# Order of the pairs in the two down projections and the mixer's output projection, and side sums added into the accumulating banks

## The chip, the cores and the metric

The kernel runs on one core of a Trainium2 chip. The metric is the device time of one execution in microseconds, as the median of several runs; lower is better. One more execution was profiled, and all rows below are from that one.

## The reference

One encoder layer on an input of 256 tokens by 2048 channels, in float32:

```
x = x + 0.5 * rms_norm((silu(a) * b) @ w_ffn1_down) * gain    # a, b = halves of rms_norm(x) @ w_ffn1_gate_up
h = rms_norm(x);  p = h @ w_mix_in                            # split into a recurrence and a window attention
x = x + rms_norm(concat(y_h, y_a) @ w_mix_out) * gain
x = x + 0.5 * rms_norm((silu(a) * b) @ w_ffn2_down) * gain    # the same again with second weights
```

The inner width of the feed-forward parts is 5632, so each down projection is a 256 x 5632 by 5632 x 2048 product; the output projection is 256 x 2048 by 2048 x 2048. Every product here is made of three: each operand is split into a high part (rounded to fp32r) and the low rest, and high x high, high x low and low x high are added.

## The kernel before

Weights stream from memory in tiles `raw` of 128 x 2048 (1 MB) through three buffers (`rawp`, L67). `split_half` makes of each half of such a tile a high part `h` on ScalarE (the cast, L168) and a low part `l` on VectorE (the subtraction, L169), in four buffers each (`hip`, `lop`, L68, L69). TensorE's results lie in the eight banks of PSUM, two tags (`pa`, `pb`) of four (L70).

The class `Pairs` (L413) runs the three projections above. The inner dimension is cut into units of 256 rows (a "pair" of 128-row blocks): 22 units in a down projection, 8 in the output projection. The 2048 output columns are done in two runs of 1024 (`begin(0)`, `begin(1)`), each over all units. One run has eight banks: four that become the result, `c[m][n]` (128 tokens by 512 columns each), and four side banks `p`.

- A **plain** unit (L462) is 8 block products into `c`, each of three matmuls: 24 matmuls of 512 columns.
- A **mixed** unit (`seven`, L468) does the same with 7 block products of sums of blocks (Strassen's scheme, Winograd's form): 21 matmuls. VectorE first makes four sums of weight blocks (`t` and a block of `raw` itself, L477 to L481); `h`, `l`, `th`, `tl` are split from those, and `sp` from sums of the left operand made earlier (`sums_of`). The tiles `t`, `th`, `tl` lie in the pool `far`, in the room of the previous stage's left operand `xt`. Four of the seven products go to the side banks `p`, three to `c`.
- The side banks reach the result through four sums `y` (`side_sums`, L511, after the first plain unit that follows the last mixed one) and four more additions `c + y` at the end of the run (`close`, L538), which also start the sum of squares for the norm on ScalarE (`jk`, L546).

In the down projections units 0, 2, ..., 16 are mixed and the order is 0 to 21, so a mixed unit comes first. In the output projection units 4 and 5 are mixed and the order is 4, 0, 5, 1, 6, 7, 2, 3.

`finish` (L574) does the second run: the last two units (`HELD`) are loaded ahead and done bank after bank (`products`), and after each bank come `close`, the product with the gain `pg` (`gains`, L602, all 2048 columns of `pg` loaded by one DMA at L586), the norm's factor `r` (`tot` L174, `v` L176 on VectorE, a power on GpSimd L178) and the update of the residual `X` (`update` L614 on VectorE, or `update_aside`, ScalarE L620 and GpSimd L621). Then `X` is turned on TensorE (L202) into the next stage's operand `xt` (high part L219 on ScalarE, low part L224 on VectorE), or stored (L632).

Outside `finish` the order on the engines is not written by hand: a scheduler at compile time orders each engine's instructions by program order and by its own model of when inputs and buffers are ready. Within the `manual_schedule` blocks of `finish` TensorE, VectorE and ScalarE keep the order of the text.

Of the kernel before, what the change touches and what calls it, by code (L numbers as in the profile page):

```python
# [36 lines left out]
def hymba_layer_kernel(  # L37
# [375 lines left out]
    class Pairs:  # L413
# [7 lines left out]
        def __init__(self, w, orders, tiles, sums, room):  # L421

            self.w, self.orders, self.tiles, self.sums = w, orders, tiles, sums
            self.room, self.post = room, None
# [7 lines left out]
        def begin(self, run):  # L432
            self.now, self.pos = run, 0
            order = self.orders[run]
            self.todo = [u for u in order if u in self.sums]
# [3 lines left out]
            some = len(self.todo)  # L439
# [6 lines left out]

        def bank(self, at):
            return self.p[at[1]] if at[0] == "p" else self.c[at[1]][at[2]]

        def three(self, at, ah, al, h, l):  # L450
            for lhs, rhs in ((ah, h), (ah, l), (al, h)):
                n = self.seen.get(at, 0)
                self.seen[at] = n + 1
                nc.tensor.matmul(  # L454
                    self.bank(at), lhs, rhs, start=(n == 0), stop=(n == self.of[at] - 1)
                )
# [54 lines left out]
        def side_sums(self):  # L511
# [16 lines left out]
            if not any(u in self.sums for u in self.orders[self.now]):  # L528
                return
            (y11, y12), (y21, y22) = y  # L530
            p1, p5, p6, p7 = self.p
            nc.scalar.copy(y11, p1)
            nc.vector.tensor_tensor(y12, p6, y11, ALU.add)
            nc.vector.tensor_tensor(y21, p7, y12, ALU.add)
            nc.vector.tensor_tensor(y12, p5, y12, ALU.subtract)
            nc.vector.tensor_tensor(y22, p5, y21, ALU.subtract)

        def close(self, m, n):  # L538
            q = 2 * self.now + n
            y = self.y[m, q]  # L540
            if any(u in self.sums for u in self.orders[self.now]):
                nc.vector.tensor_tensor(y, self.c[m][n], y, ALU.add)
            else:
                nc.vector.tensor_copy(y, self.c[m][n])
            jk = stat.tile([P, 512], BF16, tag="jk", name=nm("jk"), bufs=1)
            nc.scalar.activation(jk, y, AF.Square, accum_out=self.ssq[m][:, q : q + 1])  # L546

        def work(self, upto):

            order = self.orders[self.now]  # L550
            while self.pos < upto:
                u = order[self.pos]
                if u in self.sums:
                    self.seven(u)
                    self.todo.remove(u)
                else:
                    hs, ls = split_load(*self.source(u))
                    for k in range(2):
                        for m in range(2):
                            for n in range(2):  # L560
                                self.plain(u, hs, ls, m, n, k)
                    ready = not self.todo and (self.now == 0 or self.post)
# [794 lines left out]
```

## Time and profile before

| | us |
|---|---|
| median of 3 runs (1912.8 to 1914.1) | 1912.92 |
| the profiled execution | 1910.94 |
| its span, first to last instruction | 1909.2 |
| TensorE busy with matmuls | 1875.7 (98%) |
| VectorE busy | 1374.0 (72%) |
| ScalarE busy | 1048.9 (55%) |

The mean granted TensorE clock was 0.993 of full speed. Matmuls overlap in the profile: one of 512 columns is shown as 0.39 us long, and starts a good 0.22 us after the one before it. So TensorE's share cannot be read as work done; what is lost is seen as idle time before an instruction, or as too few matmuls in a stretch.

### The profile page before, as it was taken

To read this page: it belongs to the slowest core of one execution; us is meant where nothing else is said; L and a number is where in the kernel's file an instruction comes from. 1 tells how busy PE (TensorE), PEld (TensorE's weight loads), DVE (VectorE), ACT (ScalarE), POOL (GpSimd) and SP (SyncE) were. 2 spreads that over 40 slices of the span, in tenths; PEclk is the share of its full clock that TensorE was granted. 3 is DMA by queue.
4 is the path that set the end of the run, shared out by engine and by line. 5 is a ranking of instruction groups with operands and counts; after the bars stand their busy time and mean duration, and the time that the engine had idled before them with its cause. 6 is when DMAs were issued, how large, how long until landed. Compare 5 with 4: busy or idle time off the path is not lost.

```text
span 1909.2 us, 25425 instructions
## 1 busy us (share of the span) xinstructions
PE 1875.7 (98%) x10080; PEld 1620.0 (85%) x10080; DVE 1374.0 (72%) x1785; ACT 1048.9 (55%) x1452; POOL 38.7 (2%) x49
## 2 busy tenths in 40 slices
PE   9999999999999999999999899999999999999997
PEld 7888888888788887888888688888888888888886
DVE  6765666666698987577778787666666656598996
ACT  6544444444465656578668656544444444465553
POOL 1000000000000002000000001000000000000001
PEclk9999999999999999999999899999999999999999
DMA  7655555555465574555455455555555655465663
GB/s 245 199 196 191 188 183 193 198 177 197 156 220 199 200 285 164 199 180 165 158 182 166 148 211 199 190 186 184 192 197 176 198 191 185 155 220 200 212 252 130
DMA packets 267736, 365.92 MB, mean 192 GB/s; under 512 B 6376, under 2 KB 233792, under 8 KB 266464
## 3 DMA queue, kind: packets, MB, share of 16 engines
q1 hardware_dynamic: 267264, 364.15, 56.9%
q8 instruction: 79, 1.29, 0.3%
q14 instruction: 41, 0.34, 0.1%
q0 software_dynamic: 352, 0.14, 0.0%
HBM read 360.06 MB, written 4.21 MB: 191 GB/s over the span
## 4 chain that ended last, share of the span: by engine, by line
PE 55%; issue 41%; DVE 2%; DMA 1%; ACT 0%; POOL 0%; SPq 0%; DVEq 0%; ACTq 0%; POOLq 0%
PE pa L285 16%; PE pb L285 9%; PE pa L290 8%; PE pa L454 6%; PE pb L454 5%; PE pb L290 5%; PE pa L380 1%; PE pa L378 1%; PE pa L379 1%; DVE X L614 0%; PE pb L1094 0%; PE pb L1072 0%; PE pb L202 0%; PE pa L328 0%; DMA X<-in_x_dram 0%
## 5 line engine op out<-in xcount | busy, mean ns | idle before, releaser
L169 DVE TENSOR_TENSOR l<-raw,h 128x1024 fp32r<-128x1024 f32 x664 | 797.5, 1221 | 392.0 <-issue 288.6
L168 ACT CAST h<-raw 128x1024 fp32r<-128x1024 f32 x664 | 694.1, 1055 | 478.0 <-PE pa L285 155.7
L285 PE MATMUL pa<-xt,h 128*128 128x512 f32 x2048 | 500.2, 392 | 0.0
L285 PEld LDWEIGHTS pa<-xt,h 128*128 128x128 f32 x2048 | 375.8, 188 | 72.2
L285 PE MATMUL pb<-xt,h 128*128 128x512 f32 x1392 | 340.5, 391 | 0.0
L285 PEld LDWEIGHTS pb<-xt,h 128*128 128x128 f32 x1392 | 255.3, 188 | 49.5 <-DVE R L254 0.5
L290 PEld LDWEIGHTS pa<-xt,l 128*128 128x128 f32 x2048 | 263.5, 191 | 9.9
L290 PE MATMUL pa<-xt,l 128*128 128x256 f32 x2048 | 270.2, 284 | 0.0
L454 PE MATMUL pa<-h,ht 128*128 128x512 f32 x560 | 201.4, 392 | 5.5 <-ACT h L168 5.5
L290 PEld LDWEIGHTS pb<-xt,l 128*128 128x128 f32 x1392 | 178.5, 191 | 6.8
L290 PE MATMUL pb<-xt,l 128*128 128x256 f32 x1392 | 180.6, 283 | 0.0
L454 PE MATMUL pb<-h,ht 128*128 128x512 f32 x416 | 144.6, 389 | 0.0
L454 PEld LDWEIGHTS pa<-h,ht 128*128 128x128 f32 x560 | 105.9, 189 | 28.3 <-ACT h L168 6.4
L454 PE MATMUL pa<-l,ht 128*128 128x512 f32 x280 | 110.0, 393 | 1.1 <-DVE l L169 1.1
L454 PEld LDWEIGHTS pb<-h,ht 128*128 128x128 f32 x416 | 78.1, 188 | 16.3
L726 ACT COPY u<-pb 128x256 f32<-128x256 f32 x88 | 28.5, 376 | 110.8 <-PE pb L285 110.8
L726 ACT COPY z<-pa 128x256 f32<-128x256 f32 x88 | 28.8, 376 | 96.7 <-PE pa L285 95.8
L454 PE MATMUL pb<-l,ht 128*128 128x512 f32 x208 | 80.9, 389 | 0.0
L169 DVE TENSOR_TENSOR tl<-t,th 128x1536 fp32r<-128x1536 f32 x40 | 70.2, 1754 | 5.1 <-ACT th L168 5.0
L454 PE MATMUL pa<-h,sp 128*128 128x512 f32 x160 | 64.4, 402 | 5.1 <-ACT sp L168 4.6
L168 ACT CAST th<-t 128x1536 fp32r<-128x1536 f32 x40 | 59.2, 1481 | 13.7 <-DVE t L481 13.4
L454 PEld LDWEIGHTS pa<-l,ht 128*128 128x128 f32 x280 | 52.9, 189 | 13.0 <-DVE l L169 2.2
(245 smaller groups left out, 1705.8 us busy)
## 6 DMA issues: line engine op xcount, KB each, us to landing
raw<-in_w_ffn_gate_up_dram SPq DMA_DIRECT2D x175, 1024.0 KB, 5.0
raw<-in_w_ffn_down_dram SPq DMA_DIRECT2D x88, 1024.0 KB, 4.9
raw<-in_w_mix_in_dram SPq DMA_DIRECT2D x52, 1024.0 KB, 5.0
raw<-in_w_mix_out_dram SPq DMA_DIRECT2D x16, 1024.0 KB, 5.0
X<-in_x_dram SPq DMA_DIRECT2D x2, 1024.0 KB, 8.6
pg<-in_post_norm_ffn_dram SPq DMA_DIRECT2D x2, 1024.0 KB, 10.5
bias<-row SPq DMA_DIRECT2D x16, 128.0 KB, 3.9
kept<-X SPq DMA_DIRECT2D x2, 1024.0 KB, 4.1
```

The source lines that it names most:

```text
L168: nc.scalar.copy(hi, src)
L169: nc.vector.tensor_tensor(lo, src, hi.bitcast(F32), ALU.subtract)
L285: nc.tensor.matmul(slot[f], weights(hs, kk, f), xcol(xt, k), start=(k == 0), stop=(k == KT - 1))
L290: nc.tensor.matmul(slot[f][:, 0:T], weights(ls, kk, f), xcol(xt, kh * 8 + kk, 0), start=False, stop=False,)
L378: nc.tensor.matmul(dst, xh, h[:, o : o + n], start=(k == 0), stop=False)
L379: nc.tensor.matmul(dst, xh, l[:, o : o + n], start=False, stop=False)
L380: nc.tensor.matmul(dst, xl, h[:, o : o + n], start=False, stop=(k == KT - 1))
L454: nc.tensor.matmul(self.bank(at), lhs, rhs, start=(n == 0), stop=(n == self.of[at] - 1))
L726: nc.scalar.copy(z[:, f, :], banks[f][:, T : 2 * T])
```

## The change

1. Orders. In a down projection a plain unit comes first, then mixed and plain units in turn: 1, 0, 3, 2, 5, 4, ..., 15, 14, 17, 16, then 18 to 21 (in the second run 15, 14, 17, 16 the same, so that units under 14 stay ahead of the others). In the output projection the first run is 0, 1, 4, 6, 5, 7, 2, 3 and the second 0, 4, 1, 5, 6, 7, 2, 3.
2. `fold` replaces `side_sums`: it makes the same four sums and adds each into its bank `c[m][n]` in place, on VectorE, between the first (`after`) and the second plain unit behind the last mixed one. In those two units the products are sorted by bank, so that six matmuls of one bank stand together.
3. `close` goes. `squares` reads the bank itself on ScalarE, `gains` multiplies the bank with the gain on VectorE. The first run's gains are done at its end, and not in `finish`. `pg` is loaded in two halves, the first at the start of the first run.
4. `finish`: the same replacement within the hand-written orders; at the very end all four updates of `X[:, 0]` go to VectorE, behind `squares(1, 0)`, the last row's banks are multiplied in place in PSUM, and ScalarE with GpSimd update `X` for (1, 0) in place of (1, 3).

The number of matmuls does not change, nor that of VectorE's additions of banks (four sums and four additions a run) and of gains.

```diff
         def begin(self, run):
...
-            self.todo = [u for u in order if u in self.sums]
+            self.after = max(i for i, u in enumerate(order) if u in self.sums) + 1
...
-        def side_sums(self):
+        def half_gain(self, pool):
+            pg = pool.tile([P, 1024], F32, tag="pg", name=nm("pg"), bufs=1)
+            cs = slice(self.now * 1024, (self.now + 1) * 1024)
+            nc.sync.dma_start(pg, self.gain_src[0:1, cs].broadcast_to([P, 1024]))
+            self.pg = pg
+
+        def fold(self):
...
+            add = nc.vector.tensor_tensor
+            c = self.c
             nc.scalar.copy(y11, p1)
-            nc.vector.tensor_tensor(y12, p6, y11, ALU.add)
-            nc.vector.tensor_tensor(y21, p7, y12, ALU.add)
-            nc.vector.tensor_tensor(y12, p5, y12, ALU.subtract)
-            nc.vector.tensor_tensor(y22, p5, y21, ALU.subtract)
-
-        def close(self, m, n):
+            add(y12, p6, y11, ALU.add)
+            add(c[0][0], c[0][0], y11, ALU.add)
+            add(y21, p7, y12, ALU.add)
+            add(y12, p5, y12, ALU.subtract)
+            add(c[0][1], c[0][1], y12, ALU.add)
+            add(c[1][0], c[1][0], y21, ALU.add)
+            add(y22, p5, y21, ALU.subtract)
+            add(c[1][1], c[1][1], y22, ALU.add)
+
+        def squares(self, m, n):
+            jk = stat.tile([P, 512], BF16, tag="jk", name=nm("jk"), bufs=1)
             q = 2 * self.now + n
-            y = self.y[m, q]
-            if any(u in self.sums for u in self.orders[self.now]):
-                nc.vector.tensor_tensor(y, self.c[m][n], y, ALU.add)
...
-            nc.scalar.activation(jk, y, AF.Square, accum_out=self.ssq[m][:, q : q + 1])
+            nc.scalar.activation(
+                jk, self.c[m][n], AF.Square, accum_out=self.ssq[m][:, q : q + 1]
+            )
+
+        def gains(self, m, n, dst=None):
+            if dst is None:
+                dst = self.y[m, 2 * self.now + n]
+            nc.vector.tensor_tensor(
+                dst, self.c[m][n], self.pg[:, n * 512 : (n + 1) * 512], ALU.mult
+            )
...
                     hs, ls = split_load(*self.source(u))
...
+                    if self.pos == self.after + 1:
+                        self.fold()
+                    places = [(k, m, n) for k in range(2) for m in range(2) for n in range(2)]
+                    if self.pos in (self.after, self.after + 1):
+
+                        places.sort(key=lambda at: at[1:])
+                    for k, m, n in places:
+                        self.plain(u, hs, ls, m, n, k)
                 self.pos += 1
 
         def first_run(self):
+            self.half_gain(self.room)
             self.work(len(self.orders[0]))
             for m in range(2):
                 for n in range(2):
-                    self.close(m, n)
+                    self.squares(m, n)
+                    self.gains(m, n)
             self.begin(1)
...
+                def in_place(n):
+                    gains(1, n, dst=self.c[1][n])
+                    y[1, 2 + n] = self.c[1][n]
+
                 with tc.manual_schedule(engines=ordered):
...
+                    products(0, 0, every)
+                    squares(0, 0)
+                    gains(0, 0)
+                    products(0, 1, every)
+                    squares(0, 1)
+                    gains(0, 1)
+                    products(1, 0, every)
+                    squares(1, 0)
+                    for q in range(4):
+                        update(0, q)
+                    in_place(0)
+                    products(1, 1, every)
+                    squares(1, 1)
+                    in_place(1)
                     for q in range(4):
                         store(0, q)
-                    update_aside(1, 3)
-                    for q in range(3):
+                    update_aside(1, 0)
+                    for q in (1, 2, 3):
                         update(1, q)
                         store(1, q)
-                    store(1, 3)
+                    store(1, 0)
...
-            rows = Pairs(w_dn, [list(range(NG))] * 2, hts, sums, work)
+            plain = [u for u in range(NG) if u not in sums]
+            mixed = list(sums)
+            order = plain[:1] + [u for ab in zip(mixed, plain[1:]) for u in ab]
+            order += [u for u in plain if u not in order]
+
+            again_order = [u for u in order if u < NG - LATE] + [u for u in order if u >= NG - LATE]
+            rows = Pairs(w_dn, [order, again_order], hts, sums, work, post_gain)
...
-        rows = Pairs(w_mix_out[0], [[4, 0, 5, 1, 6, 7, 2, 3]] * 2, yt, ysums, yroom)
+        orders = [[0, 1, 4, 6, 5, 7, 2, 3], [0, 4, 1, 5, 6, 7, 2, 3]]
+        rows = Pairs(w_mix_out[0], orders, yt, ysums, yroom, post_norm_mix)
```

## Rows read from the trace of the kernel before

**Rows 1.** The page, busy time: engine, us, share of the span, instructions.

```profile
PE 1875.7 (98%) x10080; PEld 1620.0 (85%) x10080; DVE 1374.0 (72%) x1785; ACT 1048.9 (55%) x1452; POOL 38.7 (2%) x49
```

**Rows 2.** TensorE's waits, whole span: who waited <- for whom: us, times, longest.

```profile
PE pa L454 <- ACT h L168: 7.1, 3, 2.7
PE pa L454 <- ACT sp L168: 4.6, 1, 4.6
PE pa L454 <- DVE l L169: 2.1, 3, 1.0
PE pa L328 <- DVE xt L224: 1.8, 2, 1.0
PE pb L202 <- DVE X L614: 1.4, 2, 0.8
...
PE pa L202 <- DVE X L614: 0.8, 1, 0.8
PE pa L454 <- DVE sp L169: 0.5, 1, 0.5
PE pa L380 <- DVE xt L224: 0.4, 1, 0.4
```

**Rows 3.** Stretches, TensorE: from:to, length, busy (matmuls), clock, DMA share, GB/s.

```profile
503.40:516.00 12.60, 9.32 (x33) 0.86 0.31 108
1071.00:1095.00 24.00, 16.26 (x59) 0.79 0.49 176
1664.50:1680.00 15.50, 12.22 (x47) 0.89 0.39 135
516.00:560.00 44.00, 44.00 (x196) 1.00 0.60 211
```

**Rows 4.** Stretches, all engines: length, PE, PEld, DVE, ACT, POOL (instructions), clock, DMA.

```profile
516.00:560.00 44.00, 44.00 (x196) 36.38 (x195) 42.89 (x46) 28.64 (x29) 0.00 (x0) 1.00 0.60 211
...
594.00:622.00 28.00, 28.00 (x125) 23.21 (x124) 21.16 (x24) 12.44 (x13) 0.00 (x0) 1.00 0.55 193
```

**Rows 5.** First down projection's start, in time: start, us, engine, instruction, [idle before <-releaser].

```profile
498.31 0.69 DVE L477 TENSOR_TENSOR t<-raw 128x512 f32<-128x512 f32 x1 [2.16 <-PE pb L290]
...
503.71 0.65 ACT L726 COPY u<-pb 128x256 f32<-128x256 f32 x2 [8.63 <-PE pb L285]
505.50 1.05 ACT L168 CAST h<-raw 128x1024 fp32r<-128x1024 f32 x1 [1.15 <-DVE raw L478]
```

**Rows 6.** A side sum, and the switch from run 0 to run 1.

```profile
597.13 0.68 DVE L534 TENSOR_TENSOR y<-pb,y 128x512 f32<-128x512 f32 x1
...
621.12 1.28 DVE L542 TENSOR_TENSOR y<-pa,y 128x512 f32<-128x512 f32 x2
...
621.84 0.63 ACT L546 ACTIVATE jk<-y 128x512 bf16<-128x512 f32 x1 [0.52 <-DVE y L542]
622.38 0.19 ACT L546 ACTIVATION_READ_ACCUMULATOR jk<-y 128x1 f32 x1
```

**Rows 7.** End of the first down projection, in time.

```profile
732.89 0.63 ACT L546 ACTIVATE jk<-y 128x512 bf16<-128x512 f32 x1 [1.42 <-DVE y L542]
...
735.05 1.42 DVE L614 SCALAR_TENSOR_TENSOR X<-y,r,X 128x512 f32<-128x512 f32 x2 [0.46 <-POOL r L178]
```

**Rows 8.** The kernel's last 13 us, in time.

```profile
1896.82 2.41 DVE L614 SCALAR_TENSOR_TENSOR X<-y,r,X 128x512 f32<-128x512 f32 x2
...
1896.96 0.39 PE L454 MATMUL pb<-h,ht 128*128 128x512 f32 x1
...
1899.16 0.68 DVE L542 TENSOR_TENSOR y<-pb,y 128x512 f32<-128x512 f32 x1
...
1900.68 0.16 DVE L174 TENSOR_REDUCE tot<-ssqr 128x1 f32<-128x4 f32 x1 [0.85 <-ACT jk L546]
...
1902.07 3.08 DVE L614 SCALAR_TENSOR_TENSOR X<-y,r,X 128x512 f32<-128x512 f32 x3 [0.44 <-POOL r L178]
```

**Rows 9.** DMA issues: tile, queue, times, KB each, median us to landing.

```profile
pg<-in_post_norm_ffn_dram SPq DMA_DIRECT2D x2, 1024.0 KB, 10.5
```

More of the change, by code (lines that the diff above doesn't have):

```diff
@@ L438, in begin @@
             self.seen = {}
-            some = len(self.todo)
+            some = sum(u in self.sums for u in order)
             plain = len(order) - some
@@ L445, in begin @@
                 self.of["c", m, n] = 6 * plain + (3 * some if i < 3 else 0)
+            self.rest = 6 * (len(order) - self.after - 1)
         def bank(self, at):
@@ L451, in three @@
             for lhs, rhs in ((ah, h), (ah, l), (al, h)):
-                n = self.seen.get(at, 0)
-                self.seen[at] = n + 1
+                n = self.seen.get(at, 0) + 1
+                self.seen[at] = n
+                ends = self.of[at] - (self.rest if at[0] == "c" else 0)
                 nc.tensor.matmul(
-                    self.bank(at), lhs, rhs, start=(n == 0), stop=(n == self.of[at] - 1)
+                    self.bank(at),
+                    lhs,
+                    rhs,
+                    start=(n == 1),
+                    stop=n in (ends, self.of[at]),
+                    skip_group_check=n > ends,
                 )
@@ L554, in work @@
                     self.seven(u)
-                    self.todo.remove(u)
                 else:
                     hs, ls = split_load(*self.source(u))
[L558 to L562, printed above, removed]
-                    if ready and (0, 2 * self.now) not in self.y:
-                        self.side_sums()
+                    if self.pos == self.after + 1:
[5 more added lines that the diff above has]
+                        self.plain(u, hs, ls, m, n, k)
                 self.pos += 1
         def first_run(self):
+            self.half_gain(self.room)
             self.work(len(self.orders[0]))
@@ L621, in update_aside @@
                 nc.gpsimd.tensor_tensor(X[:, m, sl], X[:, m, sl], y[m, q], ALU.add)
-            for m in range(2):
-                for q in range(2):
-                    gains(m, q)
             ordered = {mybir.EngineType.PE, mybir.EngineType.DVE, mybir.EngineType.Activation}
@@ L667, in finish @@
             with tc.manual_schedule(engines=ordered):
-                for n in range(2):
-                    products(0, n, every)
-                    close(0, n)
+                products(0, 0, every)
+                squares(0, 0)
+                gains(0, 0)
+                products(0, 1, every)
+                squares(0, 1)
+                gains(0, 1)
                 products(1, 0, every)
@@ L674, in finish @@
                 update_aside(0, 2)
-                close(1, 0)
+                squares(1, 0)
+                gains(1, 0)
                 products(1, 1, slice(0, 2))
@@ L680, in finish @@
                 products(1, 1, slice(2, None))
+                squares(1, 1)
+                gains(1, 1)
                 turned(0, 1)
                 hi(0, 1)
-                close(1, 1)
                 lo(0, 1)
@@ L801, in ffn @@
             return rows.finish(
-                post_gain, mul=0.5, post=post, new_x=again, gain=gain and gain(), lead=lead
+                mul=0.5, post=post, new_x=again, gain=gain and gain(), lead=lead
             )
@@ L1269, in hymba_layer_kernel @@
         xt = rows.finish(
-            post_norm_mix,
             mul=1.0,
```

34 lines of the change are left out of this document (7 added, 27 removed).

## The prediction

> **What bounds the kernel now.** I read the busy times first: TensorE 98% of the span, no other engine above 72% [rows 1]. So time can be won only where TensorE stands or runs slowly, and lost only where something new makes it stand. The second view is TensorE's own waits. Its long ones are nearly all on line 454, the matmuls of `Pairs`: 7.1 + 4.6 + 2.1 + 0.5 = 14.3 us for `h`, `l` and `sp` [rows 2]. A second group of 1.8 + 1.4 + 0.8 + 0.4 = 4.4 us waits for `xt` and `X` in the ends of the first two projections [rows 2]. The third view, stretches of TensorE alone, gives the price of each start. In an undisturbed stretch 196 matmuls take 44.00 us, 0.2245 us each, at the full clock of 2.4 GHz [rows 3]. The starts of the three projections hold fewer: 12.60 - 33 x 0.2245 = 5.2 us lost, 24.00 - 59 x 0.2245 = 10.75 us, and 15.50 - 47 x 0.2245 = 4.95 us, together **20.9 us** [rows 3]. That is 6.6 us more than the waits, and the granted clock says why: it is 0.86, 0.79 and 0.89 there, so after standing, TensorE ran part of the stretch at 1.2 GHz [rows 3].
>
> Why a start stands is seen in the first projection's. A mixed unit comes first, and its sums need `t` in `xt`'s room, then a chain on VectorE, then the cast of `h`. ScalarE stood 8.63 us until the last copy of the previous stage at 503.71, then 1.15 us more for the sum on L478, and cast `h` only at 505.50 [rows 5]. VectorE also had 2.16 us of idle time before L477 [rows 5].
>
> **The change, part by part.**
>
> *Starts.* A plain unit needs no sums, no `far` room and no `sp`: only `raw`, the cast and the subtraction, which fit into the idle time of ScalarE and VectorE before 503.71 [rows 5]. It gives 24 x 0.2245 = 5.4 us of matmuls, the output projection's first run two such units, 10.8 us, while the chain of the mixed unit runs. In a down projection the chain held TensorE for one wait of 2.7 us and for shorter ones [rows 2]; 5.4 us should cover nearly all, though `tl` comes late in it. I leave 0.5 us of loss each (between 0 and 2.5, half of what is lost now). In the output projection the cover of 10.8 us is about as long as the 10.75 us lost; VectorE and ScalarE also finish the attention there, so I leave 1.5 us (0 to 5). Saved: 20.9 - 2 x 0.5 - 1.5 = **18.4 us**. The slow clock goes with the standing.
>
> *Fold.* Six folds (three projections, two runs). VectorE has eight operations of 0.68 us [rows 6], 5.4 us, four of which were there at this place before and four at the run's end. No row of before shows an addition written into PSUM; the nearest are those that read one bank, at 0.68 us [rows 6], and I take that. New is that TensorE waits for them. With the two units sorted by bank, a bank is complete after its six matmuls and is used again 18 matmuls later, 4.0 us. The sums can begin about 0.6 us into unit `after` (a copy on ScalarE first), so an undisturbed chain ends at 0.6 + 5.4 = 6.0 us or just after the fourth bank is complete (5.4 + 0.7 = 6.1 us). That bank is wanted at 5.4 + 18 x 0.2245 = 9.4 us. 3.3 us are left for the subtractions of the next units, which stand in the same VectorE queue; and who waits behind them is TensorE alone. What speaks against such ease is that VectorE is busy 42.89 of 44.00 us while mixed and plain units alternate [rows 4]; behind the last mixed unit it is 21.16 of 28.00 [rows 4]. Bounds: 0 (TensorE has no idle time there that a fold could remove, so nothing below) to 2 us each; I take 0.25, nearer to the undisturbed row. 6 x 0.25 = **1.5 us cost**.
>
> *Switch from run 0 to run 1.* Before, a bank was free after one addition on VectorE, 0.64 us [rows 6], and run 1 began on side banks that had long been free. Now run 1 begins with a plain unit, which wants `c[0][0]` at once, if the tiles keep their places. That bank is done 9 matmuls, 2.0 us, ahead of the switch; it must then be squared (0.63 and 0.19 us [rows 6]) and multiplied (0.68 us). Banks come every 3 x 0.2245 = 0.67 us, ScalarE needs 0.82 us for each, so the fourth is free about 4 x 0.82 + 0.68 = 4.0 us after the first was done, and is wanted at 2.0 + 9 x 0.2245 = 4.0 us. It just fits, with nothing in between; a cast of 1.05 us [rows 5] between two squares would show. I take 0.5 us (0 to 2.5) for each of three switches: **1.5 us cost**.
>
> *Gains and `pg`.* The gains are as many as before; at the end of run 0 VectorE's four gains take the place of its four additions. Nothing is added to the path. The half of `pg` enters SyncE's queue ahead of the first weight tile; 1 MB of it took 10.5 us to land [rows 9], half of it at most that. Behind it in the queue wait weight tiles, and behind those TensorE; the three `raw` buffers hold 3 x 5.4 = 16 us of TensorE's work, and DMA is at 0.31 to 0.60 of its share [rows 3]. Cost 0, and up to 5 us if the tile's room comes free late and the queue stands before it.
>
> *Ends of the first two projections.* In front of the norm's factor one addition goes; ScalarE's square stood 1.42 us waiting for it [rows 7], for the addition stood behind the gain of the bank before. `r` and so `X` come 1.4 us earlier, and the waits there are 0.8 us or less each for `X` and 1.0 us for `xt` [rows 2]. Of the 4.4 us I count 3.6 (0 to 5, with the time it takes TensorE to start again): **3.6 us**. What is late next is the chain of high and low parts of `xt`.
>
> *The kernel's end.* The last matmul starts at 1896.96 and ends at 1897.35; `tot` came at 1900.68 [rows 8], 3.33 us later, because the addition waited until 1899.16 for two updates of 1.2 us each [rows 8], made slow beside GpSimd's (0.71 us otherwise [rows 7]). After: the square follows at once, 0.1 + 0.63 + 0.19 us, and `tot` is due at 1898.3. Is VectorE free by then? Row 0's factor is due at 1897.35 - 24 x 0.2245 (two banks) + 0.9 + 1.4 (`tot` to update [rows 8]) = 1894.3; four updates of 0.71 and one gain of 0.68 end at 1897.8. Yes. From there the chain is as long as before, with three updates again [rows 8]. Gain 1900.68 - 1898.3 = 2.4; I take **2.3** (0 to 3.3).
>
> **Sum.** 18.4 + 3.6 + 2.3 - 1.5 - 1.5 = 21.3 us. Against the profiled execution: span 1909.2 - 21.3 = 1887.9. The median lies 3.7 us above that span, so 1912.9 - 21.3 = **1891.6 us**. 0.2% is 3.8 us, about what a measurement of this kernel can tell from no change.
>
> **The rivals.**
>
> (a) *The plain unit does not run ahead.* If the compile-time order keeps its casts behind the last copies, as the mixed unit's were, the first cast starts at 503.71 + 0.65 [rows 5] and not at 505.50: 1.1 us are won and perhaps 1 us of clock, 2 of 5 us in each down projection, and about half of 10.75 in the output projection. Then 9.5 in place of 18.4: 1900.5 us. Against it: the list of TensorE's waits has none on line 285, the stage ahead, which goes from tile to tile by plain casts [rows 2]. Chance 0.10.
>
> (b) *The banks at the switch.* Square and gain read the same bank on two engines; no row of before shows two engines in one bank at the same time, and the gain of before waited for the square too (it overwrote what the square read). If an operation of over 1 us stands between two of them, each switch costs 2 us, not 0.5: 1896.1 us. The Trainium skill, "PSUM — Partial Sum Buffer", Terms, says that two engines on one bank at once is an error, reads included; by that rule the two cannot overlap and the sum is as above, and if they could, the three switches would cost nothing and it would be 1890.1. Chance 0.12.
>
> (c) *The output projection stays bound by VectorE.* Its start then keeps 6.5 of 10.75 us, as the sums of two mixed units, the end of attention and the splits come together: 1896.6 us. For it speaks VectorE's 97% in the mixed stretch [rows 4]. Chance 0.12.
>
> (d) *Slower: the folds stop TensorE.* If the eight operations stand behind the next unit's subtractions and run as one block between two units, each fold costs 8 x 0.68 = 5.4 us, and slow clock as at the three starts, 6.6 / 3 = 2.2 us: 7.6 x 6 = 46 in place of 1.5: 1936 us. The change loses from (21.3 + 1.5) / 6 = 3.8 us a fold. Against it: 3.3 us of room, and VectorE idle for a quarter of the plain stretch [rows 4]. Chance 0.05.
>
> **How the numbers follow.** The forecast (1884 to 1899 by its own bounds) has 0.57, (a) 0.10, (b) 0.12, (c) 0.12, (d) 0.05; 0.04 is left for a change that moves nothing or other mishaps, half of it within 0.2%. Faster: 0.57 + 0.34 and a little = 0.91; same 0.04; slower 0.05. The range goes from all costs at zero with the ends at their upper bounds (20.9 + 5 + 3.3 = 29 us: 1883.7) to case (a) with a little more (1902): 1883 to 1902.
>
> **What the profile after would show.** TensorE's waits on line 454 for `h` and `sp` gone, the granted clock at 1.00 in the three starts; in the stretch of each fold as many matmuls as at 0.2245 us each; no wait on `c`'s banks at the switch; `tot` some 1 us behind the last matmul. Wrong would be new waits of TensorE for VectorE's `c` (the folds), for ScalarE's `jk` or VectorE's gains (the switch), or a clock below 1.00 in the middle of a run.

## The result, and the profile after

| | before | after |
|---|---|---|
| median, us (4 runs each) | 1912.86 (1912.61 to 1914.1) | 1881.42 (1881.12 to 1882.55) |
| ratio, 95% interval | | 0.9835 [0.9818, 0.9853] |
| the profiled execution, us | 1910.94 | 1881.12 |
| its span, us | 1909.2 | 1879.3 |
| mean granted TensorE clock | 0.993 | 0.999 |

The change is faster by 31.4 us, or 1.65%. The forecast was 1891.6 us with a range from 1883 to 1902: the direction was right, and the time lies 10.2 us below the forecast and 1.6 us below the range.

Where the time came from is seen by cutting both spans at the same places, the starts of the first and the last matmul of `Pairs` in each projection:

| stretch, us | before | after | saved |
|---|---|---|---|
| to the first matmul of down projection 1 | 506.60 | 503.94 | 2.66 |
| down projection 1, first to last matmul | 230.91 | 227.55 | 3.36 |
| from there to the output projection | 335.44 | 331.71 | 3.73 |
| output projection | 94.16 | 84.78 | 9.38 |
| from there to down projection 2 | 500.63 | 495.28 | 5.35 |
| down projection 2 | 229.22 | 227.08 | 2.14 |
| last matmul's start to the end | 12.20 | 8.98 | 3.22 |
| span | 1909.2 | 1879.3 | 29.9 |

TensorE's instructions come in the same number in each stretch between two projections, so the stretches can be cut further by matching them one by one. Of the 29.8 us that the rows add up to, 20.4 lie at the three starts; 5.5 at the ends of the first two projections (2.0 and 2.5 behind their last matmuls, within the first 11 us, and 1.0 in the last hundred matmuls of down projection 1, where a wait of 0.8 us on L202 stood at 735.86); 0.7 in the middle of the mixer; and 3.2 at the kernel's end. In the middle of the mixer the other kernels below that share the ends with after differ from it by 0.2 to 0.6 us too, so most of the 0.7 cannot be told from the differences between single executions.

The busy times of after, from the page (engine, us, share of the span, instructions), answer to [rows 1]. TensorE's share rose, with the same 10080 matmuls.

```profile
PE 1867.0 (99%) x10080; PEld 1617.7 (86%) x10080; DVE 1372.8 (73%) x1787; ACT 1045.2 (56%) x1450; POOL 32.5 (2%) x47
```

TensorE's waits over the whole span of after, complete, answer to [rows 2]: who waited <- for whom, us in total, times, longest. Of the 14.3 us on the matmuls of `Pairs` (L454 before, L458 now) and of the 4.4 us for `xt` and `X` one wait of 0.5 us is left. No new one has come; the one for `sc`, in the attention, was 0.2 us before.

```profile
PE pb L130 <- DVE idle L124: 1.4, 1, 1.4
PE pb L1244 <- DVE sc L1236: 0.7, 1, 0.7
PE pb L119 <- DMA rows<-in_pre_norm_ffn_dram: 0.7, 1, 0.7
PE pb L202 <- DVE X L634: 0.5, 1, 0.5
PE pb L202 <- DMA X<-in_x_dram: 0.4, 1, 0.4
```

The three starts of after as stretches of TensorE alone (from:to, length, busy (matmuls), clock, DMA share, GB/s), in the same lengths as [rows 3]: 57, 108 and 69 matmuls where there were 33, 59 and 47, all at the full 2.4 GHz. At 0.2245 us each, 57 are 12.8 us of 12.60, 108 are 24.2 of 24.00 and 69 are 15.5 of 15.50: nothing is lost there any more.

```profile
503.40:516.00 12.60, 12.60 (x57) 1.00 0.41 154
1063.00:1087.00 24.00, 24.00 (x108) 1.00 0.62 218
1643.00:1658.50 15.50, 15.50 (x69) 1.00 0.39 149
```

The first of these starts in the order of time in after (start, us, engine, instruction, idle time before and who ended it), beside [rows 5]. The plain unit's subtractions on VectorE are done at 500.02, before the stage ahead ends, so the first matmul starts at 503.94, in step with the last ones of that stage. The mixed unit's cast of `h` comes at 505.75, as late as before (505.50), and nobody waits for it.

```profile
497.66 2.36 DVE L169 TENSOR_TENSOR l<-raw,h 128x1024 fp32r<-128x1024 f32 x2 [1.26 <-issue]
...
503.94 0.39 PE L458 MATMUL pa<-h,ht 128*128 128x512 f32 x1
503.96 0.65 ACT L755 COPY u<-pb 128x256 f32<-128x256 f32 x2 [6.21 <-PE pb L285]
...
505.75 1.05 ACT L168 CAST h<-raw 128x1024 fp32r<-128x1024 f32 x1 [1.14 <-DVE raw L487]
```

A fold of the first run in after, VectorE's additions into the four banks and TensorE's first matmul of the unit behind. Twelve matmuls later, at 604.09, the third bank's turn comes, so a matmul takes 0.2267 us here. Unit `after` began 24 matmuls before 601.37, at 595.9; the last addition is done at 602.27. Its bank is wanted 18 matmuls after 601.37, at 605.45: 3.2 us of room. The first bank's addition is done at 598.21 and has 3.2 us too. The tightest is the second bank (L552), which the prediction didn't work out: its addition is done at 600.73, and it is wanted 6 matmuls after 601.37, at 602.73, so it has 2.0 us.

```profile
597.52 0.69 DVE L549 TENSOR_TENSOR pa<-pa,y 128x512 f32<-128x512 f32 x1
...
600.04 0.69 DVE L552 TENSOR_TENSOR pa<-pa,y 128x512 f32<-128x512 f32 x1
600.64 0.69 DVE L553 TENSOR_TENSOR pb<-pb,y 128x512 f32<-128x512 f32 x1
601.57 0.70 DVE L555 TENSOR_TENSOR pb<-pb,y 128x512 f32<-128x512 f32 x1 [0.24 <-PE pb L458]
...
601.37 0.39 PE L458 MATMUL pa<-h,ht 128*128 128x512 f32 x1
```

The same stretch for all engines (length, PE, PEld, DVE, ACT, POOL, clock, DMA) beside the second line of [rows 4]: TensorE has 126 matmuls where it had 125, with 3.2 us more work on VectorE.

```profile
594.00:622.00 28.00, 28.00 (x126) 23.17 (x125) 24.32 (x29) 14.88 (x20) 0.00 (x0) 1.00 0.53 188
```

The second run's fold in after has less room, since subtractions stand between its operations. The last addition is done at 718.27, and its bank is wanted at 714.92 + 18 x 0.2267 = 719.0: 0.7 us. Here too the second bank (L552) has the least: done at 715.25 + 0.69 = 715.94, wanted at 714.92 + 6 x 0.2267 = 716.28, 0.3 us. In the second runs of the other two projections it has 0.6 us.

```profile
714.92 0.39 PE L458 MATMUL pa<-h,ht 128*128 128x512 f32 x1
...
715.25 0.69 DVE L552 TENSOR_TENSOR pa<-pa,y 128x512 f32<-128x512 f32 x1
...
717.58 0.69 DVE L555 TENSOR_TENSOR pb<-pb,y 128x512 f32<-128x512 f32 x1
```

The switch from run 0 to run 1 in after, beside [rows 6]: the first square, the first matmul of run 1, and the gains. Run 1 writes its first bank at 617.68, before the first gain has begun to read (617.92). So it isn't the bank of the old result, which has still to be read: run 1's result begins in a bank that was a side bank in run 0.

```profile
616.17 0.58 ACT L560 ACTIVATE jk<-pa 128x512 bf16<-128x512 f32 x1
...
617.68 0.39 PE L458 MATMUL pa<-h,ht 128*128 128x512 f32 x1
...
617.92 1.28 DVE L567 TENSOR_TENSOR y<-pa,pg 128x512 f32<-128x512 f32 x2
```

The end of after beside [rows 8]. The last matmul ends at 1870.73 and `tot` comes at 1871.54, 0.8 us later, where it took 3.33 us. Behind the norm's factor `r`, the three updates on VectorE take 0.75 + 1.41 us and GpSimd's 1.27; before it was 3.08 us on VectorE.

```profile
1870.34 0.39 PE L458 MATMUL pb<-h,ht 128*128 128x512 f32 x1
...
1870.82 0.60 ACT L560 ACTIVATE jk<-pb 128x512 bf16<-128x512 f32 x1 [2.03 <-PE pb L458]
...
1871.54 0.16 DVE L174 TENSOR_REDUCE tot<-ssqr 128x1 f32<-128x4 f32 x1 [1.01 <-ACT jk L560]
...
1872.98 0.75 DVE L634 SCALAR_TENSOR_TENSOR X<-y,r,X 128x512 f32<-128x512 f32 x1 [0.48 <-POOL r L178]
1873.65 1.41 DVE L634 SCALAR_TENSOR_TENSOR X<-pb,r,X 128x512 f32<-128x512 f32 x2
1873.78 1.27 POOL L641 TENSOR_TENSOR X<-X,y 128x512 f32<-128x512 f32 x1 [0.83 <-ACT y L640]
```

### The profile page after: what moved, and what is told of

Its sections match the earlier page's. It is cut to its first block, busy times and chain, and to the rows that moved or that the text cites. A ratio compares the mean times of both kernels' runs of the same rounds, so it can differ in the third digit from the quotient of the medians.

```text
span 1879.3 us, 25439 instructions
## 1 busy us (share of the span) xinstructions
PE 1867.0 (99%) x10080; PEld 1617.7 (86%) x10080; DVE 1372.8 (73%) x1787; ACT 1045.2 (56%) x1450; POOL 32.5 (2%) x47
## 4 chain that ended last, share of the span: by engine, by line
PE 98%; DVE 1%; DMA 0%; ACT 0%; issue 0%; SPq 0%; DVEq 0%; POOL 0%; POOLq 0%; ACTq 0%
PE pa L285 25%; PE pb L285 17%; PE pa L458 15%; PE pb L458 14%; PE pa L290 13%; PE pb L290 9%; PE pa L380 1%; PE pa L379 1%; PE pa L378 1%; PE pb L1255 0%; PE pb L1129 0%; PE pb L1107 0%; PE pb L1191 0%; PE pa L328 0%; PE pb L202 0%; DMA X<-in_x_dram 0%
## 5 line engine op out<-in xcount | busy, mean ns | idle before, releaser
L458 PE MATMUL pa<-h,ht 128*128 128x512 f32 x560 | 198.7, 389 | 0.0
L458 PE MATMUL pb<-h,ht 128*128 128x512 f32 x416 | 143.3, 389 | 0.0
L458 PEld LDWEIGHTS pa<-h,ht 128*128 128x128 f32 x560 | 105.1, 188 | 22.0
L458 PE MATMUL pa<-l,ht 128*128 128x512 f32 x280 | 108.9, 389 | 0.0
L458 PEld LDWEIGHTS pb<-h,ht 128*128 128x128 f32 x416 | 78.1, 188 | 16.3
L458 PE MATMUL pb<-l,ht 128*128 128x512 f32 x208 | 80.9, 389 | 0.0
L458 PE MATMUL pa<-h,sp 128*128 128x512 f32 x160 | 62.2, 389 | 0.0
L458 PEld LDWEIGHTS pa<-l,ht 128*128 128x128 f32 x280 | 52.6, 188 | 10.9
```

Of the source, the lines that this page charges most:

```text
L458: nc.tensor.matmul(self.bank(at), lhs, rhs, start=(n == 1), stop=n in (ends, self.of[at]), skip_group_check=n > ends,)
```

## The experiments

The ten runs fall into four questions: how far one execution of before stands for the others, what each part is worth alone, whether the charges for folds and switches were really zero, and what the first units of the output projection do.

### The kernel before, once more

The prediction turned a span into a median with a constant. This run is the unchanged kernel before, to see whether that holds.

> The kernel before once more, so that each of its timed runs shows its span and clock. The timed median of before (1912.9) lay 1.95 us above the profiled execution (1910.94), the one of after 0.3 us above its own (1881.42 and 1881.12). Theory A: the timed runs of before differ in the slow clock behind its three standing starts, so spans lie between 1909 and 1911.5 us, and the longer ones have the lower clock. Theory B: the time around the span differs from run to run; then spans agree within 0.3 us and the clock too.

Ten executions gave 1910.94 to 1915.43 us, median 1913.09, at 1.0003 [0.9994, 1.0012] of the runs beside it. The time around the span is 1.7 to 1.9 us in every one; what spreads is the span itself, 1909.2 to 1913.7 with a median of 1911.3. So the 3.7 us that the prediction put between its span and the median were 1.8 us around the span and about 2 us by which the profiled execution (1909.2) was a short one. After spreads less, from 1879.3 to 1880.8 in span (four executions). The mean clock (0.992 to 0.994) doesn't follow the span clearly. In the profiled execution of this run the wait for `sp` is 4.9 us (4.6 in [rows 2]) and the one for the first DMA 1.3 us (0.8 in before); why the spans differ by up to 4.5 us is otherwise open.

### The new orders alone

The kernel before with the new orders, and `side_sums`, `close`, `gains` and the end as before.

```diff
-            rows = Pairs(w_dn, [list(range(NG))] * 2, hts, sums, work)
+            plain = [u for u in range(NG) if u not in sums]
+            mixed = list(sums)
+            order = plain[:1] + [u for ab in zip(mixed, plain[1:]) for u in ab]
+            order += [u for u in plain if u not in order]
+            again_order = [u for u in order if u < NG - LATE] + [u for u in order if u >= NG - LATE]
+            rows = Pairs(w_dn, [order, again_order], hts, sums, work)
...
-        rows = Pairs(w_mix_out[0], [[4, 0, 5, 1, 6, 7, 2, 3]] * 2, yt, ysums, yroom)
+        orders = [[0, 1, 4, 6, 5, 7, 2, 3], [0, 4, 1, 5, 6, 7, 2, 3]]
+        rows = Pairs(w_mix_out[0], orders, yt, ysums, yroom)
```

> The new orders alone; side sums, additions at the run's end, gains and ends as before. Theory A (the starts are worth all that the trace of after shows there, 21.5 us of span, and need nothing of the fold): span 1887.7, median 1889 to 1891. Theory B (as predicted, some of each start stays): 18.4 us, median 1894.5. Theory C (the orders pay only with the fold, for the side sums would collide with the additions at the run's end): 15 us or less, median 1898 or more.

1889.59 us, 0.9879 [0.9862, 0.9895]; span 1888.0, so 21.2 us less than the profiled execution of before. By place, 20.3 of them lie at the three starts, nearly all of the 20.9 us that [rows 3] shows as lost there. Another 1.0 lies in the last hundred matmuls of down projection 1: the wait of 0.8 us on L202 that stood there before (`pa L202` in [rows 2]) is gone with the orders alone. TensorE's waits of this kernel, in the columns of [rows 2], have none on L454, and the others of the two projections' ends stand as before:

```profile
PE pa L328 <- DVE xt L224: 2.0, 2, 1.2
...
PE pb L202 <- DVE X L614: 1.4, 2, 0.8
...
PE pa L380 <- DVE xt L224: 0.4, 1, 0.4
```

Its output projection takes 84.79 us (after: 84.78) and its end 12.19 us (before: 12.20). So starts and the rest can be told apart.

### Everything but the orders

After with the orders of before.

```diff
-            rows = Pairs(w_dn, [order, again_order], hts, sums, work, post_gain)
+            rows = Pairs(w_dn, [list(range(NG))] * 2, hts, sums, work, post_gain)
...
-        orders = [[0, 1, 4, 6, 5, 7, 2, 3], [0, 4, 1, 5, 6, 7, 2, 3]]
+        orders = [[4, 0, 5, 1, 6, 7, 2, 3]] * 2
```

> The fold, the squares and gains from the banks and the new ends, with the orders of before (a mixed unit first). Theory A (folds and switches cost nothing, ends are worth 5.1 us and the kernel's end 3.2): 8.3 us, span 1900.9, median 1904.5. Theory B (as predicted: 3.6 and 2.3 us less 3.0 of cost): 2.9 us, median 1910. A wait of TensorE for a bank in the middle of a run would speak for B.

1902.7 us, 0.9949 [0.9934, 0.9964]; span 1900.3, 8.9 us less than before's. Together with the orders' 21.2 that is 30.1, and the whole change saved 29.9. By the medians the parts gain 22.7 and 9.6 us, 32.3 together, where the change gained 31.4. So the two parts add up to within about 1 us. The starts' waits are back in TensorE's list:

```profile
PE pa L458 <- ACT h L168: 7.1, 3, 2.7
PE pa L458 <- ACT sp L168: 4.9, 1, 4.9
PE pa L458 <- DVE l L169: 2.7, 4, 1.0
```

One thing was not expected. The first start of this kernel and that of the run of before stand through the same wait of 2.75 us, yet the clock afterwards is not the same. First TensorE's first matmul of `Pairs` and the stretch (columns of [rows 3]) in this kernel, then both in the repeated run of before:

```profile
506.85 0.50 PE L458 MATMUL pa<-h,ht 128*128 128x512 f32 x1 [2.75 <-ACT h L168]
...
503.60:518.00 14.40, 10.46 (x44) 1.00 0.43 145
```

```profile
507.32 0.50 PE L454 MATMUL pa<-h,ht 128*128 128x512 f32 x1 [2.75 <-ACT h L168]
...
503.60:518.00 14.40, 11.12 (x44) 0.88 0.41 144
```

The first down projection takes 229.3 us here, 230.9 and 230.6 in the two traces of before. Only 0.6 us of that difference lies in this start. At the full clock TensorE came sooner to the next product and had to wait for its `l`: at 510.45 it stood 0.67 us, the fourth wait for `l` in the list above, where [rows 2] has three. The other 0.7 to 1.0 us lie in the last hundred matmuls, where the wait on L202 is gone here as well. So 0.6 us of this kernel's 8.9 are slow clock that didn't come, and the 1.0 us at that end is counted in both parts, since either of them alone removes the wait.

### The old end

After with the last block of `finish` in the order of before (without the addition of the side sums, which has gone).

```diff
-                    products(0, 0, every)
-                    squares(0, 0)
-                    gains(0, 0)
...
-                    for q in range(4):
-                        update(0, q)
-                    in_place(0)
...
+                    for m in range(2):
+                        products(m, 0, every)
+                        squares(m, 0)
+                        gains(m, 0)
+                        if m == 1:
+                            update(0, 0)
+                            update_aside(0, 2)
+                            update(0, 1)
+                            update_aside(0, 3)
+                        products(m, 1, every)
+                        squares(m, 1)
+                        gains(m, 1)
...
-                    update_aside(1, 0)
-                    for q in (1, 2, 3):
+                    update_aside(1, 3)
+                    for q in range(3):
```

> The changed kernel with the old order at the kernel's very end: two of row 0's updates on ScalarE and GpSimd, the last row's gains into SBUF and (1, 3) aside, but no addition any more. Theory A (the gain at the end, 3.2 us, comes from the order: VectorE's updates slow beside GpSimd's hold the last gain and the factor): 2 to 3 us slower than the changed kernel, 1883.4 to 1884.4. Theory B (it comes from the addition that is gone, as the square no longer waits for VectorE): under 1 us slower.

1883.35 us, 0.9848 [0.9833, 0.9862]; span 1881.5. From the last matmul's start to the end it takes 10.47 us, between before (12.20) and after (8.98), so it lies between the two theories. Of the 3.2 us, 1.7 came with the addition that is gone and 1.5 with the new order and the last gains left in PSUM, which this kernel undoes together. Two rows of its end show the second part: the norm's `tot` waits behind the updates of the other row until 1872.46 (last matmul's start at 1871.02; 1.44 us, in after 1.20), and the three updates beside GpSimd take 3.08 us, as in [rows 8].

```profile
1872.46 0.14 DVE L174 TENSOR_REDUCE tot<-ssqr 128x1 f32<-128x4 f32 x1
...
1874.20 3.08 DVE L634 SCALAR_TENSOR_TENSOR X<-y,r,X 128x512 f32<-128x512 f32 x3 [0.81 <-POOL r L178]
```

### The folds: without the sorting, and with VectorE delayed

Three kernels ask whether the folds cost nothing because of the sorting by bank, because of the room of 3.3 us, or by luck. These three and the kernels after them were each run once and are set against the profiled execution of after; after's own spans differ by 1.5 us, so less than that tells nothing by itself, and the waits tell more. The first leaves the products of the two units in the order of all others:

```diff
-                    if self.pos in (self.after, self.after + 1):
-                        places.sort(key=lambda at: at[1:])
```

> The changed kernel without the sorting by bank in the two units around the fold. Each bank is then complete 9 matmuls, 2.0 us, before it is used again, and not 18, 4.1 us. Theory A (the sort is what hides the fold): the chain of eight operations of 0.68 us is late by 1 us and more, six times, so span 1885 to 1890 and waits of TensorE for VectorE's banks. Theory B (VectorE has room enough, the sort is not needed): span within 1 us of 1879.3.

1881.58 us (one execution; after 1881.12 to 1882.55), span 1879.8, and no wait that after doesn't have. The order on VectorE adapted: it makes the four sums first and then adds into the banks one behind the other, at 599.58, 600.26, 600.94 and 601.62. Here the last bank is wanted after 9 matmuls of the next unit, at 601.42 + 9 x 0.2267 = 603.46, and its addition ends at 602.32. It has 1.1 us of room, and so has each of the other three: less than the 2.0 us of the tightest bank with the sorting, and still enough. In the second runs TensorE's matmuls stand in another order as well, so the compile-time order makes room on both engines.

The second and the third put 4 and 10 additions more in front of each fold's sums on VectorE (each takes the maximum of `y11` with itself, which changes nothing).

```diff
             nc.scalar.copy(y11, p1)
+            for _ in range(4):      # 10 in the third kernel
+                add(y11, y11, y11, ALU.max)
             add(y12, p6, y11, ALU.add)
```

> The changed kernel with four more VectorE operations of 512 columns (each an idle maximum of y11 with itself, 2.7 us in all) ahead of each fold's first sum. Theory A (as predicted, the last bank's addition has 3.3 us of room; the trace of after shows 3.2 in the first run): no wait of TensorE, span 1879 to 1880. Theory B (the fold just fits): each fold 1 to 2.7 us late, span 1885 to 1895.

1885.35 us (one execution), span 1883.6, 4.3 us more than after. The first runs' three folds show no wait, those of the second runs 1.8, 0.5 and 1.1 us. TensorE's wait in the columns of [rows 2], and the longest one:

```profile
PE pa L458 <- DVE pa L551: 3.4, 3, 1.8
...
716.56 0.47 PE L458 MATMUL pa<-h,ht 128*128 128x512 f32 x1 [1.79 <-DVE pa L551]
```

Neither theory is right for all six. In the first run 4 x 0.68 = 2.7 us are more than the second bank's room of 2.0, and yet nothing waits, because TensorE's order changed too: two matmuls on a `pb` bank now stand ahead of the second bank's, which start at 602.84, just behind their addition (done at 602.59). In the second run the late bank is the first, `c00`: in after its addition is done at 711.73 + 0.69 = 712.42 and it is wanted at 714.92, 2.5 us of room; here two subtractions slip in front as well, the sums begin 4.0 us later (715.12 in place of 711.13), and TensorE stands.

> The same with ten, 6.8 us in all, twice the room. Theory A: the first bank's addition comes after TensorE wants it, by 2 to 3.6 us in each of six folds; span 1891 to 1900, with waits of TensorE for VectorE's pa, and a clock below 1.00 behind some. Theory B (the compile-time order moves the fold or other work and takes up anything): span within 2 us of 1879.3.

1938.28 us (one execution), span 1936.4, 57.1 us more than after, far over what either theory gave it. All six folds stop TensorE, by 5.4 to 8.9 us. The wait in total; then what VectorE did in the first fold (two subtractions for the next units, 1.22 us each, stayed in front of the sums) and the first matmul that waited; then the stretch (columns of [rows 3]).

```profile
PE pa L458 <- DVE pa L551: 41.4, 6, 8.9
...
603.69 1.22 DVE L169 TENSOR_TENSOR l<-raw,h 128x1024 fp32r<-128x1024 f32 x1
...
605.42 1.22 DVE L169 TENSOR_TENSOR l<-raw,h 128x1024 fp32r<-128x1024 f32 x1
...
607.99 0.76 PE L458 MATMUL pa<-h,ht 128*128 128x512 f32 x1 [5.41 <-DVE pa L551]
...
602.00:614.00 12.00, 6.59 (x19) 0.72 0.25 89
```

Ten additions are 6.8 us; less the room of 3.2 that is 3.6, and with the two subtractions up to 6.0, where 5.41 was measured. On top comes TensorE's clock: 0.72 in this stretch, after standing. 57.1 / 6 = 9.5 us a fold, of which 6.9 (41.4 / 6) is waiting. So a fold that is late by more than its room does cost what rival (d) feared; the one of the change isn't late.

### The banks at the switch

In after, run 1 doesn't begin on the banks that run 0 has just finished, so the switch of the prediction was not tried by it. This kernel forces it: four clears give run 1's side banks the rooms that come free early, and its results must take the old result banks.

```diff
+            if run:
+                for bank in self.p:
+                    nc.vector.memset(bank, 0.0)
```

> The changed kernel in which VectorE zeroes the four side banks of run 1 at the switch, so that they take the banks that are free first and the result's banks must take those that squares and gains still read. (The zeros are overwritten by the first matmul.) Theory A (the switch was free because run 1's result starts in the old side banks): each of three switches now waits 0.9 to 1.5 us, span 1882 to 1884. Theory B (squares and gains are fast enough anyway): span within 0.7 us of 1879.3. Rival (b) of the prediction, 2 us each: span 1885.

1882.36 us (one execution), span 1880.5; no wait of TensorE at the switches. Of the 1.2 us over after, 0.9 lie ahead of the first projection and in the mixer, and 0.3 in the three projections with the switches. VectorE's clear of the first freed bank, its first gains, and two matmuls of TensorE:

```profile
599.23 0.48 DVE L450 MEMSET pb<- 128x512 f32 x1
...
617.53 1.28 DVE L570 TENSOR_TENSOR y<-pa,pg 128x512 f32<-128x512 f32 x2
...
618.13 0.39 PE L461 MATMUL pa<-h,sp 128*128 128x512 f32 x1
618.35 0.41 PE L461 MATMUL pa<-h,ht 128*128 128x512 f32 x1
```

The compile-time order answered too: matmuls of the mixed unit (the one at 618.13 has `sp` as an operand) stand ahead of the plain unit's, whose first starts at 618.35, and the first gain ends at 618.2. That its result took the old result banks fits this, since each of the first three banks is written 0.1 to 0.3 us behind its gain's end. The fourth gain ends at 620.56 + 0.68 = 621.24. If the plain unit's matmuls had stood in their own order from 617.9 on, the fourth bank would have been wanted 9 matmuls later, at 619.9, and TensorE would have stood 1.3 us at most. So the price at a switch is between 0, as run, and 1.3 us by this working.

### The first units of the output projection

After with other first runs in the output projection: a mixed unit first (the list of before), and one plain unit first in place of two.

```diff
-        orders = [[0, 1, 4, 6, 5, 7, 2, 3], [0, 4, 1, 5, 6, 7, 2, 3]]
+        orders = [[4, 0, 5, 1, 6, 7, 2, 3], [0, 4, 1, 5, 6, 7, 2, 3]]      # mixed first
+        orders = [[0, 4, 1, 5, 6, 7, 2, 3], [0, 4, 1, 5, 6, 7, 2, 3]]      # one plain
```

> The changed kernel, but the output projection's first run in the old order 4, 0, 5, 1, 6, 7, 2, 3. Theory A (this one start is worth 11 us): span 1890 to 1891, with the waits of TensorE for h, l and sp, 7 to 8 us, back. Theory B (the plain start of the other projections shifts the work so that less is lost here): 1884 to 1888.

1893.63 us (one execution), span 1891.8. The output projection takes 94.02 us (before 94.16, after 84.78) and the stretch ahead of it 333.37 (after 331.71): 10.9 us. Of these 0.6 lie in the middle of the mixer and 10.3 at this start, close to the 10.75 that the prediction read from [rows 3]. The other 1.6 us are a later first matmul of the first down projection (505.56), a stretch that this edit doesn't touch. TensorE's waits of this kernel on `Pairs`:

```profile
PE pa L458 <- ACT sp L168: 4.8, 1, 4.8
PE pa L458 <- ACT h L168: 1.6, 1, 1.6
```

> The same with one plain unit ahead (0, 4, 1, 5, 6, 7, 2, 3) in place of two. Theory A (VectorE and ScalarE are late by more than one unit there, as case (c) of the prediction had it for two): 2 to 5 us slower than with two, span 1881.5 to 1884.5, TensorE waiting for sp or tl. Theory B (one plain unit, 5.4 us, covers the chain): span within 1 us of 1879.3.

1886.1 us (one execution), span 1884.2, 4.9 more than after. 1.6 us of them lie in the output projection (86.35 us, after 84.78); 1.4 are at the kernel's start, 1.1 in the first down projection and 0.5 in the mixer, places that this edit doesn't touch. So 1.6 us is what one plain unit fails to cover, a little less than theory A had, and two cover all. TensorE's waits:

```profile
PE pa L458 <- DVE pa L552: 0.8, 1, 0.8
...
PE pb L458 <- DVE tl L169: 0.7, 1, 0.7
```

The second line is the price in the output projection: `tl`, late as the prediction said of it. The first is a fold, in the first down projection's second run, in code that is the same as in after. It is the second bank's (L552), the one with 0.3 us of room; ScalarE had waited 1.64 and 1.66 us there for weight tiles, and this fold's sums began 2.9 us into unit `after`, where it was 1.6 in after. That the late tiles are the cause was not tried. So that fold is close, and in some executions it may cost something.

## Why the prediction was right in its mechanisms and short in its size

The bound was read rightly: TensorE's standing and its slow clock at three starts, the ends, and the kernel's end are where nearly all the time came from. The gains of three terms were sized too small, two charges too large, and one conversion was wrong; with 0.7 us in the mixer they make the 10.2 us.

**Starts, 18.4 forecast, 20.3 measured** (new orders alone, by place; 20.4 in after). The loss of 20.9 was read well. What failed is the remainder of 2.5 us, left because "`tl` comes late" and because VectorE and ScalarE finish the attention: a plain unit covered the chain in each down projection, two covered it in the output projection. The doubt was not idle. With one plain unit `tl` is late by 0.7 us. Rivals (a) and (c) fall too: in after the plain unit runs ahead (first matmul at 503.94, in step), and the output projection's start holds 108 matmuls in 24.00 us. That the 6.6 us beyond the listed waits are the slow clock was borne out in part only: at the full clock one of these starts was 0.6 us shorter, and a wait costs TensorE more than the list shows (see the ends below). How the 6.6 divide is open.

**Folds, 1.5 us charged, none found.** The working was close to the trace: the last addition ends 6.3 us after unit `after` begins (worked out: 6.1), an addition into PSUM takes 0.69 to 0.70 us (taken: 0.68), the room is 3.2 us (3.3). With its own numbers the step gave zero, and I charged 0.25 a fold as a precaution. The prediction treated all six folds alike and worked out the last bank only; the second bank has 2.0 us in the first runs and 0.3 to 0.6 in the second, and only second runs' folds stopped TensorE in the kernel with four more additions and in the one with one plain unit. Rival (d) has its mechanism (9.5 us a fold when late) but not its condition.

**Switches, 1.5 us charged, none found**, and for another reason than those weighed: the condition "if the tiles keep their places" was false, and run 1 begins on old side banks, as before. Where the condition was forced, no wait came either, as the compile-time order moved matmuls. Rival (b) falls. The Trainium skill, "PSUM — Partial Sum Buffer", Terms, has it that two engines on one bank at once is an error, reads included; the trace agrees as far as it goes, since each gain begins after its bank's square has ended (616.75 and 617.92 for the first), and no run here shows the two at once.

**Ends of the first two projections, 3.6 forecast, 5.5 measured** (2.0, 2.5 and 1.0, by place). The mechanism came as said: with the new orders alone the first high part of `xt` starts at 731.60, 0.2 us behind the last matmul's start, and in after at 730.53, 1.0 us ahead of it. The step that failed is the size, taken from the waits alone and then lowered. Of the 4.4 us of waits [rows 2] 3.9 went, and each cost more than it shows, as these two rows of the new orders alone tell:

```profile
737.38 0.40 PE L380 MATMUL pa<-h,xt 128*128 128x512 f32 x1
738.54 0.66 PE L202 MATMUL pb<-ident,X 128*128 128x128 f32 x4 [0.76 <-DVE X L614]
```

Between the two starts lie 1.16 us, and 0.23 in after: the wait is listed as 0.76 and cost 0.93, since the list counts idle time only from the shown end of the matmul ahead. The upper bound of 5 was too low for the same reason.

**The kernel's end, 2.3 forecast, 3.2 measured.** The `tot` step came as predicted (2.4 by its working, 3.33 - 0.81 = 2.5 in the trace), though [rows 8] doesn't show "two updates of 1.2 us each": of the two, the first took 0.75 us and the second, which began while GpSimd's addition ran, 1.75. The step that failed is "from there the chain is as long as before, with three updates again": with two of the three reading `y` from PSUM they took 2.1 us and not 3.08, and GpSimd's 1.27 and not 1.74.

**From span to median.** "The median lies 3.7 us above that span" was taken as a constant of the kernel. 1.8 us of it are. The other 1.9 are one short execution among many: the profiled span of before lies that much below the median of its spans (1912.9 - 1.8 = 1911.1), that of after only 0.3 us (1881.4 - 1.8 = 1879.6 against 1879.3). So the medians gain 31.4 us where the profiled spans gain 29.9, 1.6 us of the miss.

In sum: 2.0 (starts) + 3.0 (folds and switches) + 1.9 (ends) + 0.9 (end) + 0.7 (the mixer, not forecast) + 1.6 (conversion) = 10.1 us, the miss but for rounding. The low end of the range, 1883, was the corner where all charges are zero, 1883.7, rounded down. By the prediction's own conversion 1883 stands for 29.9 us of gain, and that is what the profiled spans show; that the parts meet it so closely is chance. The 1.6 us by which the median lies below the range are the conversion, as the spread of before was not counted at all.

Gains and `pg` cost nothing, as said: after has no wait for a weight tile in `Pairs`.

## What to carry to other kernels

When a step's own arithmetic leaves microseconds of room, charge zero for it and put the precaution into the range; small charges on every edit add up to a bias (here about 5 of 10.2 us). Where work that needs a long chain on other engines opens a stage, put a piece that needs only its own load in front of it, and choose how many by the length of the chain: one plain unit of 5.4 us was enough in two stages, two were needed in the third. Count the room of each copy of a repeated step, not of one: the tightest bank of the same fold had 2.0 us in one run and 0.3 in the other, and the second is the sensitive one.

## What the runs showed of the hardware that was not expected

- An update of `X` on VectorE with both its tensors in SBUF that began while GpSimd's addition to `X` ran took 1.75 us, and one that began just before GpSimd's took 0.75, like one alone; so the 3.08 us for three in before and with the old end are 0.75 + 0.75 + 1.75, overlapped a little, and not 1.03 each. With `y` in PSUM, in after, the update that began while GpSimd's ran took 0.74 us. GpSimd's own addition took 1.27 us there and 1.74 beside the first kind. No run changed the place of `y` alone.
- Adding in place into a PSUM bank costs VectorE no more than reading one: 0.69 to 0.70 us for 512 columns against 0.68, and TensorE goes on accumulating in that bank afterwards.
- The same wait of 2.75 us at the same start was followed by a granted clock of 0.88 in a stretch of before and of 1.00 in the kernel with all but the orders, so the slow clock behind such a wait isn't certain; in the stretch with a wait of 5.41 us it was 0.72.
